# Wide products for every pair of parts two and three of a SwiGLU FFN, like products grouped, and the first corner cleared earlier

## The chip, the cores and the metric

One core of one Trainium2 chip runs the whole program. The metric is the device time of one execution in microseconds; three executions of the kernel before took 1763.86, 1764.16 and 1764.58 us, and their median, 1764.16 us, is what the change is compared with.

## The reference

Two layers of an encoder trunk on 512 tokens of width 1024, in float32. Each layer merges three token mixers, adds the result to x, and then runs the part that the change touches, a SwiGLU FFN (`D_FF` is 2816, so 22 blocks of 128 hidden channels), followed by a gated embedding:

```python
for i in range(DEPTH):
    h = rmsnorm(x, norm_mix[i])
    ...                                   # three mixers, merged; x = x + merged @ w_o[i]
    h = rmsnorm(x, norm_ffn[i])
    x = x + (jax.nn.silu(h @ w_ffn_gate[i]) * (h @ w_ffn_up[i])) @ w_ffn_down[i]
    h = rmsnorm(x, norm_ple[i])
    x = x + jax.nn.sigmoid(h @ w_ple_gate[i]) * (p[i] @ w_ple_in[i])
return rmsnorm(x, norm_final)
```

## The kernel before

**Arithmetic.** A float32 product is made of fp32r products: each operand is split into a high part (a copy in fp32r) and a low part (the rest), and a product is the sum of three, high weights with high activations, high weights with low activations, and low weights with high activations. ScalarE (ACT) makes the high part, VectorE (DVE) the low one (`split`, L143 and L157 for every operation of its kind). In a plain `gemm` the three are L179, L180 and L181, each 512 tokens wide.

**The FFN.** `ffn` goes through the 22 blocks `fb` in three parts, of 8, 7 and 7 blocks. For each block, a *pair* (gate block and up block), `seven` computes gate and up together by seven products in place of eight: the weights are taken as a 2x2 matrix (`a11`, `a12` of the gate block, sums `s1` to `s4`, `a22`), the activations as a 2x2 matrix too (`b11`, `b21`, `b22` and the differences `t1` to `t4`), over two halves of the channels and two halves of the 512 tokens. A product runs over four steps `k` of 128 channels and is 256 tokens wide. After a part's pairs, its block results go through the rows of `w_ffn_down` as plain gemms.

**Narrow and wide products.** In a pair with even `fb`, a product step is three matmuls of 256 columns (L1011, L1012, L1013), all into one 256-wide accumulator. In a pair with odd `fb` (`twice`), the high weights meet the high and the low activations in one matmul of 512 columns (L1008), into an accumulator of two halves, and the low weights meet the high activations in one of 256 columns (L1009) into the first half; the two halves are added when the accumulator is read. The product `T` (`s1` with `t3`) is narrow in every pair, so a wide pair has six wide products and a narrow one. Reading a two-half accumulator costs a copy on ACT and an addition on DVE that a narrow one doesn't have.

**Accumulators.** A pair has three in PSUM. `C` takes `a11 b11`; ACT copies it to `A`; `C` then takes `a12 b21` as well and is the first corner of the result (the gate for the first token half). `A` takes `s3 t2`, is copied by ACT to `Q`, takes `s2 t1`, is read out by ACT (`self.cleared`), and takes `s4 b22`; `Q` takes `a22 t4`. Even pairs hold three banks called `mm`, odd pairs two called `sc` and one called `av`, so a bank comes free for the next pair but one. The first pair of all (`fb` 0, `early`) does `s4 b22` apart.

**Order.** TensorE's (PE) order is written by hand: `sevens_of` runs two pairs interleaved, so that between `s2 t1` of a pair and its `s4 b22` stand two other products (its own `a22 t4`, and `T` of the next pair), and between its corner `a12 b21` and the next use of that bank, by `a11 b11` of the next pair but one, stand six. The other engines' orders come from the scheduler of the tile framework, by priority (weights are hoisted), with a few orders forced by `behind`. SP issues the weight DMAs, POOL the accumulating DMAs (L976) that form `s1` and `s2`. Tiles: `wr` raw weights, `wh` and `wl` their parts, `qk` the sums, `pt` and `y` the parts of `s3`, `s4` for even and odd pairs, `kh` and `a` those of `a22`, `t` results, `h`, `rp`, `b`, `v`, `z` the activations.

Of the kernel before, what the change touches and what calls it, by code (L numbers as in the profile page):

```python
# [20 lines left out]
P = 128  # L21
# [40 lines left out]
class Net:  # L62
# [212 lines left out]

    def norm_chunk(self, k, x, g, tag, st, n=512):

        if k == KD - 1:
            self.sumsq(k, x, st)
        if n < 512:  # L280
            tag = self.sb(tag, [P, 2, 512], F32R)[:, :, :n]
        h = self.operand(x[:, :n], g, tag)
        if k < KD - 1:
            self.sumsq(k, x, st)
        return h
# [616 lines left out]
    def w_o(self, mg, xsrc):  # L902
        self.phase = "wo"
        xs, h, st, self.four = [], [], [], []
        self.zs = [self.parts_of("z", [2, 256], 2, F32R) for _ in range(4)]
        for m in range(KD):
            if m % 2 == 0:
                two = self.parts_of("x", [512], 2)
            xo = two[m % 2]
            self.nc.sync.dma_start(xo, xsrc[m])  # L910
            if m == 0:
                both = [self.ps("mm") for _ in range(2)]
                self.pair(both, self.a["w_o"][self.i, 0:2], mg)
# [6 lines left out]
            h.append(self.norm_chunk(m, xo, self.par(self.i, "ffn", m), "h", st, 512 if m % 2 else 256))  # L920
# [40 lines left out]
    def seven(self, wg, wu, bs, tags, spare, md, first, fb, early, twice):  # L961


        nc = self.nc
        with self.tc.high_priority(offset=min(self.w_ahead, self.tc.cur_priority - self.p0)):
# [30 lines left out]
            self.tt(s4, s3, g[:, up], ALU.add)  # L996
            halve(*spare, sums[1], ("s3", "s4"))
        shape = (P, 2, 256) if twice else (P, 256)
        C, A, Q = (self.ps(t, shape) for t in tags)

        def product(out, w, b, first=False):
            wh, wl = ws[w]
            mm = nc.tensor.matmul
            for k in range(4):
                c = slice(k * P, k * P + P)
                both = bs[k][b]
                if len(out.shape) > 2:
                    mm(out, wh[:, c], both, start=first and k == 0, stop=False, skip_group_check=True)  # L1008
                    mm(out[:, 0], wl[:, c], both[:, 0], start=False, stop=k == 3, skip_group_check=True)  # L1009
                    continue  # L1010
                mm(out, wh[:, c], both[:, 0], start=first and k == 0, stop=False, skip_group_check=True)  # L1011
# [20 lines left out]
        product(T, "s1", "t3", True)  # L1032
        shared = gg[:, 1] if twice else uu[:, 0]
        self.act(shared, T, AF.Copy)
# [7 lines left out]
        if twice:  # L1042
            self.act(uu[:, 1], A[:, 0], AF.Copy)
            self.cleared = self.act(gg[:, 0], A[:, 1], AF.Copy)
        else:
            self.cleared = self.act(uu[:, 1], A, AF.Copy)
        product(Q, "a22", "t4")
        if twice:
            self.tt(uu[:, 1], uu[:, 1], gg[:, 0], ALU.add)
            self.act(uu[:, 0], Q[:, 1], AF.Copy)  # L1050
            self.tt(uu[:, 0], Q[:, 0], uu[:, 0], ALU.add)
            self.tt(uu, uu, gg[:, 1:2].to_broadcast([P, 2, 256]), ALU.add)
        else:
# [68 lines left out]
    def ffn(self, h, x):  # L1122
# [5 lines left out]
        md8 = [self.sb(t, [P, 2, 512], F32R) for t in ["v"] * 3 + ["z"] + ["y"] * 3]  # L1128
        md8.append(tuple(self.sb("e", [P, 512], F32R) for _ in range(2)))
        self.sums, self.sevens = [t for _ in range(2) for t in self.parts_of("qk", [1024], 2)], 0  # L1130
        for part in PARTS:
            mids = md8[:len(part)]
            self.sevens_of((self.seven(self.a["w_fg"][i, fb], self.a["w_fu"][i, fb], bs,
                                       (("mm", "mm", "mm"), ("sc", "sc", "av"))[fb % 2],
                                       spare[fb % 2], md8[f], part[0] and f < 2, fb, fb == 0,
                                       fb % 2 == 1)
                            for f, fb in enumerate(part)), part[0] == 0)
# [368 lines left out]
```

## Time and profile before

| what | value |
|---|---|
| three executions | 1763.86, 1764.16, 1764.58 us |
| profiled execution, its own time | 1764.9 us |
| its span on the core | 1763.1 us (1.8 us of the time lie outside it) |
| DVE busy in the span | 1388.2 us (79%) |
| ACT busy in the span | 934.6 us (53%) |
| granted TensorE clock | 0.999 |

The span holds three stretches of pairs in each layer, with the gemms of `w_ffn_down` behind each: in the first layer pairs of part one from 491 to 572.2 us, of part two from 615.8 to 685.6, of part three from 723.7 to 793.4; in the second layer each about 873 us later. Records of matmuls overlap, since they are pipelined: what a matmul costs is the distance from its start to the next one's, not its duration. In the rows below, a tile's name has its stage ahead of it (`ffn_mm`), and `out<-in` says what is written and from what.

### The profile page before, as it was taken

Reading aid. Unit: us, or ns where it says so; the run is one execution under the profiler, and the core shown is the slowest. Engines: PE = TensorE matmul, PEld = TensorE weight load, DVE = VectorE, ACT = ScalarE, POOL = GpSimd, SP = SyncE. Lnnn points to the kernel's source line nnn. Section 1 sums busy time; section 2 is a strip of 40 time slices with the busy share of each in tenths; the row PEclk is TensorE's granted clock in tenths of the full one; section 3 lists DMA queues with packets and bytes.
Section 4 is the critical chain, followed back from the end, with each engine's and each line's share of the span. In section 5 each row is a group of like instructions: output and inputs, shape, how many; then the busy total and the mean of one; then the engine's idle time right before and its main releaser. Section 6 shows DMA issues by size and latency. Waiting matters only on the chain.

```text
span 1763.1 us, 26202 instructions
## 1 busy us (share of the span) xinstructions
PE 1756.3 (100%) x9618; PEld 1525.2 (87%) x9618; DVE 1388.2 (79%) x2264; ACT 934.6 (53%) x1649; POOL 104.1 (6%) x114
## 2 busy tenths in 40 slices
PE   9999999999999999999999999999999999999998
PEld 7889888888899898898888888888888998989987
DVE  7967988998788676777776789889887875877776
ACT  5566555326576264464545655552356653645554
POOL 0000000000121020100000000000001210201000
PEclk9999999999999999999999999999999999999999
DMA  6565641334767365543445655322356664656332
GB/s 227 163 188 157 164 123 54 102 99 150 223 161 181 119 170 154 141 118 131 149 137 166 190 148 153 111 75 93 101 182 190 180 166 122 177 143 154 97 105 96
DMA packets 114785, 253.90 MB, mean 144 GB/s; under 512 B 16864, under 2 KB 23776, under 8 KB 114656
## 3 DMA queue, kind: packets, MB, share of 16 engines
q1 hardware_dynamic: 101264, 227.83, 41.9%
q0 software_dynamic: 12672, 23.07, 8.0%
q8 instruction: 76, 1.25, 0.3%
q10 hardware_dynamic: 720, 1.31, 0.2%
q14 instruction: 53, 0.43, 0.1%
HBM read 215.46 MB, written 7.34 MB: 126 GB/s over the span
## 4 chain that ended last, share of the span: by engine, by line
PE 99%; DVE 0%; ACT 0%; POOL 0%; issue 0%; POOLq 0%; ACTq 0%; DVEq 0%
PE ffn_sc L1008 6%; PE ffn_mm L179 4%; PE ffn_mm L180 4%; PE ffn_mm L181 4%; PE ffn_mm L1011 4%; PE ffn_mm L1013 4%; PE ffn_mm L1012 4%; PE ffn_sc L1009 3%; PE mergea_mm L179 2%; PE mergea_mm L181 2%; PE mergea_mm L180 2%; PE diff_sc L798 2%; PE diff_mm L179 2%; PE diff_mm L180 2%; PE gatec_mm L180 2%; PE natten_mm L180 2%
## 5 line engine op out<-in xcount | busy, mean ns | idle before, releaser
L160 DVE SCALAR_TENSOR_TENSOR conv_z<-glu_z,pre_par,conv_z 128x512 f32<-128x512 f32 x240 | 179.4, 748 | 3.4
L143 ACT ACTIVATE ffn_wh<-ffn_wr 128x1024 fp32r<-128x1024 f32 (+1 forms) x92 | 92.6, 1020 | 117.1 <-PE ffn_mm L180 61.4
L157 DVE TENSOR_TENSOR ffn_wl<-ffn_wr,ffn_wh 128x1024 fp32r<-128x1024 f32 (+1 forms) x92 | 107.1, 1175 | 40.2 <-ACT ffn_wh L143 39.7
L976 POOL DMA_DIRECT2D ffn_qk<-w_fu x88 | 78.0, 974 | 595.6 <-DMA ffn_qk<-w_fu 308.0
L157 DVE TENSOR_TENSOR ffn_t<-ffn_mm,wo_rb 128x512 f32<-128x512 f32 (+1 forms) x86 | 47.9, 557 | 55.1 <-PE ffn_mm L181 46.9
L143 ACT ACTIVATE mergea_wh<-mergea_wr 128x1024 fp32r<-128x1024 f32 (+1 forms) x32 | 27.1, 846 | 96.8 <-PE mergea_mm L180 79.5
L157 DVE TENSOR_TENSOR ffn_t<-ffn_t,ffn_t 128x512 f32<-128x512 f32 x88 | 54.4, 619 | 18.0 <-ACT ffn_t L143 18.0
L157 DVE TENSOR_TENSOR ffn_wl<-ffn_qk,ffn_wh 128x1024 fp32r<-128x1024 f32 x44 | 53.8, 1223 | 16.6 <-ACT ffn_wh L143 16.6
L1008 PE MATMUL ffn_sc<-wo_h,ffn_wh 128*128 128x512 f32 x176 | 64.2, 399 | 0.1
L143 ACT ACTIVATE ffn_wh<-ffn_qk 128x1024 fp32r<-128x1024 f32 x44 | 46.6, 1060 | 31.4 <-PE ffn_mm L180 16.2
L143 ACT ACTIVATE diff_a<-diff_sc,diff_s 128x512 f32<-128x512 f32 x32 | 22.1, 689 | 70.8 <-DVE diff_s L891 70.8
L181 PE MATMUL ffn_mm<-ffn_v,ffn_wl 128*128 128x512 f32 x132 | 51.4, 390 | 0.0
L180 PE MATMUL ffn_mm<-ffn_v,ffn_wh 128*128 128x512 f32 x132 | 51.4, 390 | 0.0
L179 PE MATMUL ffn_mm<-ffn_v,ffn_wh 128*128 128x512 f32 x132 | 51.3, 389 | 0.0
L179 PE MATMUL ffn_mm<-ffn_y,ffn_wh 128*128 128x512 f32 x132 | 51.3, 389 | 0.0
L180 PE MATMUL ffn_mm<-ffn_y,ffn_wh 128*128 128x512 f32 x132 | 51.3, 389 | 0.0
L181 PE MATMUL ffn_mm<-ffn_y,ffn_wl 128*128 128x512 f32 x132 | 51.3, 389 | 0.0
L1011 PE MATMUL ffn_mm<-wo_h,ffn_wh 128*128 128x256 f32 x176 | 50.0, 284 | 0.0
L1012 PE MATMUL ffn_mm<-wo_h,ffn_wh 128*128 128x256 f32 x176 | 49.8, 283 | 0.0
L1013 PE MATMUL ffn_mm<-wo_h,ffn_wl 128*128 128x256 f32 x176 | 49.8, 283 | 0.0
L1009 PE MATMUL ffn_sc<-wo_h,ffn_wl 128*128 128x256 f32 x176 | 49.5, 281 | 0.0
L143 ACT ACTIVATE natten_wh<-natten_wr 128x1024 fp32r<-128x1024 f32 x24 | 25.4, 1058 | 42.1 <-issue 15.2
(847 smaller groups left out, 6325.4 us busy)
## 6 DMA issues: line engine op xcount, KB each, us to landing
ffn_qk<-w_fu POOLq DMA_DIRECT2D x88, 256.0 KB, 6.3
ffn_wr<-w_fg SPq DMA_DIRECT2D x44, 512.0 KB, 4.4
ffn_wr<-w_fd SPq DMA_DIRECT2D x32, 448.0 KB, 4.0
ffn_r<-w_fu SPq DMA_DIRECT2D x44, 256.0 KB, 3.3
ffn_qk<-w_fg SPq DMA_DIRECT2D x44, 256.0 KB, 3.2
ffn_qk<-w_fu SPq DMA_DIRECT2D x44, 256.0 KB, 3.4
natten_wr<-w_in SPq DMA_DIRECT2D x16, 512.0 KB, 4.0
diff_wr<-w_in SPq DMA_DIRECT2D x16, 512.0 KB, 4.2
```

The source lines that it names most:

```text
L143: i = self.nc.scalar.activation(out, in_, func, **kw)
L157: return self.nc.vector.tensor_tensor(out, a, b, op)
L160: return self.nc.vector.scalar_tensor_tensor(out, a, s, b, op0, op1)
L179: mm(out, wh, ah, start=first, stop=False, **kw)
L180: mm(out, wh, al, start=False, stop=False, **kw)
L181: mm(out, wl, ah, start=False, stop=last, **kw)
L976: nc.gpsimd.dma_start(q, wu[:, lo], accum_op=ALU.add)
L1008: mm(out, wh[:, c], both, start=first and k == 0, stop=False, skip_group_check=True)
L1009: mm(out[:, 0], wl[:, c], both[:, 0], start=False, stop=k == 3, skip_group_check=True)
L1011: mm(out, wh[:, c], both[:, 0], start=first and k == 0, stop=False, skip_group_check=True)
L1012: mm(out, wh[:, c], both[:, 1], start=False, stop=False, skip_group_check=True)
L1013: mm(out, wl[:, c], both[:, 0], start=False, stop=k == 3, skip_group_check=True)
```

## The change

Four edits, all in the FFN.

1. `twice`, which makes a pair's products wide, is true for all pairs of parts two and three, and no longer only for odd `fb`. Those are 7 more pairs in each layer, 14 in all.
2. In a wide product the four matmuls of the high weights come first, one for each `k`, and then the four of the low weights. Before, the two kinds alternated.
3. A wide pair gets two side tiles (`side`, from the ring `e`) for the second half of `A` and for `T`. With these free, the first corner `C` is read out and added right behind its last product, where it was read at the pair's end together with `A`. The reading of `A` at the end is kept in `self.late`, and the low parts of `s3` and `s4` of the next pair but one are put behind it on DVE.
4. The normalised activations `h` are laid out as token half, then high or low, so that `b11`, `b21` and `b22` are each one contiguous piece of 512 columns; before they were two pieces of 256.

```diff
+            h.append(self.sb("h", [P, 2, 2, 256], F32R))
+            self.norm_chunk(m, xo, self.par(self.i, "ffn", m), h[m], st, m % 2 + 1)
...
-        return dict(b11=ha, b21=hb[:, :, one], b22=hb[:, :, two],
+        return dict(b11=ha[:, 0], b21=hb[:, 0], b22=hb[:, 1],
...
-            halve(*spare, sums[1], ("s3", "s4"))
+            i = halve(*spare, sums[1], ("s3", "s4"))
+            if self.late[fb % 2] is not None:
+                self.behind(i, self.late[fb % 2])
+                self.late[fb % 2] = None
...
-                if len(out.shape) > 2:
-                    mm(out, wh[:, c], both, start=first and k == 0, stop=False, skip_group_check=True)
-                    mm(out[:, 0], wl[:, c], both[:, 0], start=False, stop=k == 3, skip_group_check=True)
-                    continue
+            if len(out.shape) > 2:
+                for k, c in enumerate(cols):
+                    mm(out, wh[:, c], bs[k][b], start=first and k == 0, stop=False,
+                       skip_group_check=True)
+                for k, c in enumerate(cols):
+                    mm(out[:, 0], wl[:, c], bs[k][b][:, 0], start=False, stop=k == 3,
+                       skip_group_check=True)
...
         def corner():
             product(C, "a12", "b21")
-            if not early and not twice:
+            if twice:
+                self.act(gg[:, 0], C[:, 1], AF.Copy)
+                self.tt(gg[:, 0], C[:, 0], gg[:, 0], ALU.add)
+            elif not early:
                 self.tt(gg[:, 0], C, self.halved(0), ALU.mult)
...
-            self.cleared = self.act(gg[:, 0], A[:, 1], AF.Copy)
+            self.cleared = self.act(side[:, 1], A[:, 1], AF.Copy)
...
-            for n, o in enumerate((C, A)):
-                self.act(gg[:, n], o[:, 1], AF.Copy)
-                self.tt(gg[:, n], o[:, 0], gg[:, n], ALU.add)
+            self.act(gg[:, 1], A[:, 1], AF.Copy)
+            self.late[fb % 2] = self.tt(gg[:, 1], A[:, 0], gg[:, 1], ALU.add)
...
+        side = [self.sb("e", [P, 2, 256]) for _ in range(2)]
...
-                                       fb % 2 == 1)
+                                       fb, fb == 0, fb % 2 == 1 or part[0] > 0)
```

The first place is on PE, in part two: the product `s4 b22` of pair 10 into its accumulator `A` (`ffn_mm_1110_6464` before, `ffn_mm_1112_6432` now; `wo_h` are the activations, `ffn_pt` the parts of `s4`). Before:

```order
L1011 MATMUL ffn_mm_1110_6464<-wo_h_802_4422,ffn_pt_871_4766 128x256
L1012 MATMUL ffn_mm_1110_6464<-wo_h_802_4422,ffn_pt_871_4766 128x256
L1013 MATMUL ffn_mm_1110_6464<-wo_h_802_4422,ffn_pt_872_4767 128x256
L1011 MATMUL ffn_mm_1110_6464<-wo_h_822_4522,ffn_pt_871_4766 128x256
L1012 MATMUL ffn_mm_1110_6464<-wo_h_822_4522,ffn_pt_871_4766 128x256
L1013 MATMUL ffn_mm_1110_6464<-wo_h_822_4522,ffn_pt_872_4767 128x256
L1011 MATMUL ffn_mm_1110_6464<-wo_h_844_4625,ffn_pt_871_4766 128x256
L1012 MATMUL ffn_mm_1110_6464<-wo_h_844_4625,ffn_pt_871_4766 128x256
L1013 MATMUL ffn_mm_1110_6464<-wo_h_844_4625,ffn_pt_872_4767 128x256
L1011 MATMUL ffn_mm_1110_6464<-wo_h_862_4725,ffn_pt_871_4766 128x256
L1012 MATMUL ffn_mm_1110_6464<-wo_h_862_4725,ffn_pt_871_4766 128x256
L1013 MATMUL ffn_mm_1110_6464<-wo_h_862_4725,ffn_pt_872_4767 128x256
```

Now, with the lines of the changed kernel (L1013 is the wide matmul, L1016 the narrow one):

```order
L1013 MATMUL ffn_mm_1112_6432<-wo_h_802_4422,ffn_pt_871_4766 128x512
L1013 MATMUL ffn_mm_1112_6432<-wo_h_822_4522,ffn_pt_871_4766 128x512
L1013 MATMUL ffn_mm_1112_6432<-wo_h_844_4625,ffn_pt_871_4766 128x512
L1013 MATMUL ffn_mm_1112_6432<-wo_h_861_4722,ffn_pt_871_4766 128x512
L1016 MATMUL ffn_mm_1112_6432<-wo_h_802_4422,ffn_pt_872_4767 128x256
L1016 MATMUL ffn_mm_1112_6432<-wo_h_822_4522,ffn_pt_872_4767 128x256
L1016 MATMUL ffn_mm_1112_6432<-wo_h_844_4625,ffn_pt_872_4767 128x256
L1016 MATMUL ffn_mm_1112_6432<-wo_h_861_4722,ffn_pt_872_4767 128x256
```

Twelve matmuls of 256 columns have become four of 512 and four of 256; the columns that stream are the same 3072. All in all PE has 336 matmuls fewer (84 products, four fewer in each).

The second place is on ACT, in part two, around the reading of pair 8's `A` (`ffn_mm_1082_6230` before, `ffn_mm_1084_6216` now) ahead of its `s4 b22`. Before:

```order
L143 ACTIVATE ffn_sc_1096_6351<-ffn_sc_1095_6350 128x512
L143 ACTIVATE ffn_wh_1103_6447<-ffn_wr_1101_6439 128x1024
L143 ACTIVATE ffn_v_876_4771<-ffn_t_1070_6119 128x512
L143 ACTIVATE ffn_kh_1105_6451<-ffn_r_1102_6440 128x512
L143 ACTIVATE ffn_t_1085_6233<-ffn_mm_1082_6230 128x256
L143 ACTIVATE ffn_t_1098_6353<-ffn_tr_1100_6391 128x256
```

Now, for the same pair:

```order
L143 ACTIVATE ffn_sc_1098_6324<-ffn_sc_1097_6323 128x512
L143 ACTIVATE ffn_wh_1105_6415<-ffn_wr_1103_6407 128x1024
L143 ACTIVATE ffn_v_876_4771<-ffn_t_1072_6110 128x512
L143 ACTIVATE ffn_kh_1107_6419<-ffn_r_1104_6408 128x512
L143 ACTIVATE ffn_t_1087_6219<-ffn_mm_1084_6216 128x256
L143 ACTIVATE ffn_e_884_4779<-ffn_mm_1084_6216 128x256
L143 ACTIVATE ffn_t_1087_6219<-ffn_mm_1085_6217 128x256
L143 ACTIVATE ffn_e_885_4780<-ffn_tr_1102_6359 128x256
```

The four operations ahead of the reading of `A` are the same; the reading itself is now two copies, and a copy of the second half of `Q` stands behind them.

The third place is on DVE at the beginning of the first layer's FFN, between the reading of pair 1's accumulators and the parts of pair 2's and 3's weights (`ffn_sc_913_4911` is pair 1's `C` before, `ffn_sc_915_4913` now). Before:

```order
L157 TENSOR_TENSOR ffn_wl_938_5127<-ffn_wr_935_5118,ffn_wh_937_5126 128x1024
L157 TENSOR_TENSOR ffn_t_917_4915<-ffn_t_917_4915,ffn_t_916_4914 128x256
L157 TENSOR_TENSOR ffn_pt_872_4767<-ffn_qk_885_4780,ffn_pt_871_4766 128x1024
L157 TENSOR_TENSOR ffn_a_940_5131<-ffn_r_936_5119,ffn_kh_939_5130 128x512
L157 TENSOR_TENSOR ffn_qk_885_4780<-ffn_qk_884_4779,ffn_r_936_5119 128x512
L157 TENSOR_TENSOR ffn_t_917_4915<-ffn_av_915_4913,ffn_t_917_4915 128x256
L157 TENSOR_TENSOR ffn_qk_885_4780<-ffn_qk_885_4780,ffn_wr_935_5118 128x512
L157 TENSOR_TENSOR ffn_t_917_4915<-ffn_t_917_4915,ffn_t_916_4914 128x512
L157 TENSOR_TENSOR ffn_t_916_4914<-ffn_sc_913_4911,ffn_t_916_4914 128x256
```

Now:

```order
L157 TENSOR_TENSOR ffn_t_918_4916<-ffn_sc_915_4913,ffn_t_918_4916 128x256
L157 TENSOR_TENSOR ffn_qk_887_4782<-ffn_qk_887_4782,ffn_wr_923_5001 128x512
L157 TENSOR_TENSOR ffn_wl_940_5129<-ffn_wr_937_5120,ffn_wh_939_5128 128x1024
L157 TENSOR_TENSOR ffn_a_942_5133<-ffn_r_938_5121,ffn_kh_941_5132 128x512
L157 TENSOR_TENSOR ffn_pt_872_4767<-ffn_qk_887_4782,ffn_pt_871_4766 128x1024
L157 TENSOR_TENSOR ffn_t_919_4917<-ffn_t_919_4917,ffn_e_885_4780 128x256
L157 TENSOR_TENSOR ffn_qk_887_4782<-ffn_qk_886_4781,ffn_r_938_5121 128x512
```

The reading of pair 1's `C` has moved from the last of these rows to the first, ahead of pair 3's first weight parts; and pair 2's low part of `s3` and `s4` (`ffn_pt_872`) now stands behind `ffn_a`, the low part of `a22`, where it stood ahead of it. The DMA issues of SP and POOL stand in the same order as before.

More of the change, by code (lines that the diff above doesn't have):

```diff
@@ L957, in quarters, with seven @@
         ha, hb = h[2 * j], h[2 * j + 1]
-        return dict(b11=ha, b21=hb[:, :, one], b22=hb[:, :, two],
+        return dict(b11=ha[:, 0], b21=hb[:, 0], b22=hb[:, 1],
                     **{f"t{n + 1}": o for n, o in enumerate(d)})
-    def seven(self, wg, wu, bs, tags, spare, md, first, fb, early, twice):
+    def seven(self, wg, wu, bs, tags, spare, side, md, first, fb, early, twice):
         nc = self.nc
@@ L1032, in seven @@
         product(T, "s1", "t3", True)
-        shared = gg[:, 1] if twice else uu[:, 0]
+        shared = side[:, 0] if twice else uu[:, 0]
         self.act(shared, T, AF.Copy)
@@ L1134, in ffn @@
                                        (("mm", "mm", "mm"), ("sc", "sc", "av"))[fb % 2],
[L1135 to L1136 removed]
+                                       spare[fb % 2], side[fb % 2], md8[f], part[0] and f < 2,
+                                       fb, fb == 0, fb % 2 == 1 or part[0] > 0)
                             for f, fb in enumerate(part)), part[0] == 0)
```

20 lines of the change are left out of this document (11 added, 9 removed).

## The prediction

> **What bounds the kernel now.** I read the page's span and its chain of waits first.
>
> ```profile
> span 1763.1 us, 26202 instructions
> ...
> PE 99%; DVE 0%; ACT 0%; POOL 0%; issue 0%; POOLq 0%; ACTq 0%; DVEq 0%
> ```
>
> The chain that ended last lies on PE for 99% of the span, so what counts is how far apart matmuls start. I read that next from windows with exact borders, in the first layer: the gemms behind part one, then the pairs of part two, then those of part three.
>
> ```profile
> core 0: us, PE busy (x) PEld busy (x) DVE busy (x) ACT busy (x) POOL busy (x), PEclk, DMA share, GB/s
> 572.23:615.78 43.55, 43.55 (x194) 36.04 (x193) 27.97 (x37) 12.14 (x16) 0.00 (x0) 1.00 0.37 120
> 615.79:685.62 69.83, 69.83 (x517) 66.54 (x516) 54.30 (x82) 45.50 (x79) 12.40 (x14) 1.00 0.68 167
> 723.74:793.37 69.63, 69.63 (x493) 65.25 (x492) 52.80 (x80) 45.31 (x80) 7.04 (x8) 1.00 0.51 134
> ```
>
> The counts in brackets include one or two matmuls that cross a border; by the code they are 192, 516 and 492. The 192 of the gemms have 512 columns each: 43.55 / 192 = 226.8 ns. Part two has four narrow pairs and three wide ones: 4 x 84 + 3 x 12 = 372 narrow matmuls, and 3 x 24 = 72 steps of a wide and a narrow one. Part three has 3 x 84 + 4 x 12 = 300 and 96. With n for a narrow matmul and p for a wide-and-narrow step, 372 n + 72 p = 69.83 and 300 n + 96 p = 69.63, so n = 119.8 ns and p = 351.0 ns. The timeline shows a wide product in single rows, from 565.19 to 566.60:
>
> ```profile
> 565.19 0.40 PE L1008 MATMUL ffn_sc<-wo_rp,ffn_y 128*128 128x512 f32 x1
> 565.42 0.28 PE L1009 MATMUL ffn_sc<-wo_rp,ffn_y 128*128 128x256 f32 x1
> 565.54 0.40 PE L1008 MATMUL ffn_sc<-wo_rp,ffn_y 128*128 128x512 f32 x1
> 565.78 0.28 PE L1009 MATMUL ffn_sc<-wo_rp,ffn_y 128*128 128x256 f32 x1
> 565.90 0.40 PE L1008 MATMUL ffn_sc<-wo_z,ffn_y 128*128 128x512 f32 x1
> 566.14 0.28 PE L1009 MATMUL ffn_sc<-wo_z,ffn_y 128*128 128x256 f32 x1
> 566.25 0.40 PE L1008 MATMUL ffn_sc<-wo_z,ffn_y 128*128 128x512 f32 x1
> ...
> 566.60 0.40 PE L1008 MATMUL ffn_sc<-wo_h,ffn_wh 128*128 128x512 f32 x1
> ```
>
> From n and the gemms, 256 more columns cost 226.8 - 119.8 = 107 ns, so that a matmul costs 12.8 ns beside its columns. That is all a wide product can save, since the columns stay the same.
>
> **Term 1, 84 products become wide.** A narrow product is 12 x 119.8 = 1437.6 ns, a wide one as it is now 4 x 351.0 = 1404.0 ns. 14 pairs x 6 products x 33.6 ns = **2.8 us less**.
>
> **Term 2, like matmuls grouped, in 132 + 84 = 216 wide products.** A wide-and-narrow step takes 351.0 ns where 226.8 + 119.8 = 346.6 would do: alternating costs 4.4 ns a step. Grouped, a product alternates once and not four times: 3 x 4.4 = 13.2 ns, x 216 = **2.9 us less**; if that once goes too, 3.8 us. On the bad side, the rows let the excess be the wide matmul's own: three wide ones start 0.23, 0.24 and 0.24 us ahead of their narrow ones (236.7 ns mean), and three narrow ones take 0.12, 0.12 and 0.11. If wide ones keep 236.7 ns and narrow ones in a row take 119.8, a product is 1426 ns, 22 ns more than now, 4.8 us in all. I take 2.9, because the gemms' matmuls, of the same size and in a row, hold 226.8 ns over 192 of them.
>
> **The operands in one piece: nothing.** The half-and-half `wo_h` and the one-piece `wo_rp` take the same already:
>
> ```profile
> L1008 PE MATMUL ffn_sc<-wo_h,ffn_wh x176: 387/398/468, 498.6 to 1662.0; 128*128 128x512 f32 x176
> L1008 PE MATMUL ffn_sc<-wo_rp,ffn_wh x44: 393/397/404, 509.1 to 1662.7; 128*128 128x512 f32 x44
> ```
>
> **Term 3, the waits at the FFN's beginning.** PE waits twice in a layer in its first 30 us of pairs, and not behind that:
>
> ```profile
> 517.55 0.28 PE L1013 MATMUL ffn_mm<-wo_h,ffn_wl 128*128 128x256 f32 x1
> 517.86 0.47 PE L1008 MATMUL ffn_sc<-wo_h,ffn_wh 128*128 128x512 f32 x1
> ...
> 523.50 0.28 PE L1013 MATMUL ffn_tr<-wo_z,ffn_wl 128*128 128x256 f32 x1
> 523.79 0.39 PE L1011 MATMUL ffn_mm<-wo_h,ffn_pt 128*128 128x256 f32 x1
> ```
>
> ```profile
> 513.42 1.22 DVE L157 TENSOR_TENSOR ffn_pt<-ffn_qk,ffn_pt 128x1024 fp32r<-128x1024 f32 x1
> ...
> 517.29 0.42 DVE L157 TENSOR_TENSOR ffn_t<-ffn_sc,ffn_t 128x256 f32<-128x256 f32 x1
> ```
>
> The first (0.31 us between starts where 0.12 is usual, and 0.07 more in the longer matmul: 0.26) is pair 3's first product, which needs the bank of pair 1's `C`: DVE reads that at 517.29 and is done at 517.71. Early clearing puts this reading some six us ahead (the third place in the order), so the wait goes. The second (0.29 for 0.12, and 0.11 in the matmul: 0.28) is pair 2's `s4 b22`, which needs `A` read by ACT; in the new order the copy and the Silu that delayed ACT stand ahead of it, and I let it go too. What is late next is the low part of `s3` for pair 2: it ends at 514.64, and its first reader starts at 515.03:
>
> ```profile
> 515.03 0.29 PE L1013 MATMUL ffn_mm<-wo_rp,ffn_pt 128*128 128x256 f32 x1
> ```
>
> That is 0.39 us of room, and the new order puts the low part of `a22` ahead of it (0.60 us from start to start; the addition of 0.33 that stood there has gone behind, the reading of `C` of 0.33 has come ahead). I take a new wait of 0.14, between 0 and 0.3. A layer gains 0.26 + 0.28 - 0.14 = 0.40, two layers **0.8 us**; ends 0 and 1.1.
>
> **What is added beside PE.** Each of the 14 pairs gets two additions of 256 columns turned into ones of 512 and two more of 256 on DVE, on ACT four more copies of 256 and two that grow to 512. The groups of part two give the prices (417 and 685 ns; on ACT 378 and 582):
>
> ```profile
> L157 DVE TENSOR_TENSOR ffn_t<-ffn_sc,ffn_t 128x256 f32<-128x256 f32 x6 | 2.5, 417 | 0.5 <-ACT ffn_t L143 0.5
> L157 DVE TENSOR_TENSOR ffn_t<-ffn_t,ffn_t 128x512 f32<-128x512 f32 x9 | 6.2, 685 | 0.8 <-ACT ffn_t L143 0.8
> L143 ACT ACTIVATE ffn_t<-ffn_sc 128x256 f32<-128x256 f32 x12 | 4.2, 378 | 2.5 <-DVE ffn_t L157 1.5 <-PE ffn_sc L1009 1.1
> L143 ACT ACTIVATE ffn_sc<-ffn_sc 128x512 f32<-128x512 f32 x3 | 1.7, 582 | 0.4 <-PE ffn_sc L1009 0.4
> ```
>
> DVE: 2 x 0.417 + 2 x 0.268 = 1.37 us a pair, in part two 54.30 + 4 x 1.37 = 59.8 of 69 us, 87%. ACT: 4 x 0.378 + 2 x 0.204 = 1.92, 45.50 + 7.7 = 53.2 of 69, 77%. Neither becomes the pace; PE's work hides them, and it costs nothing as long as no product waits. The low parts of `s3` and `s4`, now forced behind the reading of `A`, are due late: in the steady part DVE makes them some seven us ahead of use. DMA issues keep their order.
>
> The tightest place is the reading of `A` by ACT ahead of `s4 b22`, in the steady part:
>
> ```profile
> 644.06 0.28 PE L1012 MATMUL ffn_mm<-wo_z,ffn_wh 128*128 128x256 f32 x1
> ...
> 647.15 0.28 PE L1011 MATMUL ffn_mm<-wo_h,ffn_pt 128*128 128x256 f32 x1
> ```
>
> ```profile
> 644.38 1.06 ACT L143 ACTIVATE ffn_wh<-ffn_wr 128x1024 fp32r<-128x1024 f32 x1 [0.55 <-PE ffn_mm L1012]
> 645.35 0.62 ACT L143 ACTIVATE ffn_v<-ffn_t 128x512 fp32r<-128x512 f32 x1
> 645.87 0.62 ACT L143 ACTIVATE ffn_kh<-ffn_r 128x512 fp32r<-128x512 f32 x1
> 646.39 0.36 ACT L143 ACTIVATE ffn_t<-ffn_mm 128x256 f32<-128x256 f32 x1
> ...
> 655.36 0.64 ACT L143 ACTIVATE ffn_t<-ffn_sc 128x256 f32<-128x256 f32 x2
> ```
>
> The last high matmul of `s2 t1` (644.06 to 644.34) frees the buffer that ACT then fills with the next high weights (644.38), behind which stand three more operations; `A` is free at 646.75, and PE wants it at 647.15: 0.40 us of room. Now, from the start of the last high matmul: it lasts 0.40, so ACT starts at +0.44, the first copy of `A` 2.01 later, and both copies take 0.64 (the row of two at 655.36): free at +3.09. PE wants `A` when `s2 t1` has ended, four narrow matmuls and one wide later (0.71), and `a22 t4` (1.39) and `T` (1.44) have run: +3.54. The room is 0.45 us. No wait is added.
>
> **The sum.** 2.8 + 2.9 + 0.8 = 6.5 us less. The rows are those of one execution of 1764.9 us (its span 1763.1 and 1.8 around it), which becomes 1758.4; the median of the runs, 1764.16, lies 0.7 lower, and I take the same 6.5 from it: **1757.7 us**. The ends of the terms are 7.7 less (1756.5) and 2.8 - 4.8 + 0 = 2.0 more (1766.2).
>
> **Rivals.** *Grouping brings nothing*, because the 4.4 ns belong to the pair of matmuls on the same columns and not to the change of width. For: no row before shows wide matmuls of this form in a row. Against: the gemms' 226.8. It leaves 2.8 + 0.8: 1760.6 us. Chance 0.19.
>
> *Columns alone set the pace*: merging two matmuls then saves nothing, and grouping neither; only term 3 stays, 1763.4 us. Against it stands n: 119.8 is more than half of 226.8, and p less than 3 n. Chance 0.06. The Trainium skill (TensorE: Matmul & The Clock Gate, Back-to-back issue gap) comes close to this case: it states a gap of N / 2.4 + 2.5 ns for a warm matmul, so 2.5 ns beside the columns. By that, an estimate from the page, term 1 would be 84 x 4 x 2.5 ns = 0.84 us, and the time 1762.5 us with term 3. The trace differs, with 12.8 ns.
>
> *`A` is read too late* in the 28 pairs of parts two and three of both layers: now two copies must be through before `s4 b22`. If ACT's first operation of the chain starts later, by more than 0.45 us, PE waits in every pair. If another hi part of 1024 columns (0.97 us from 644.38 to 645.35) gets ahead, each pair waits 0.97 - 0.45 = 0.52, 28 x 0.52 = 14.6 us: 1772.3 us. It decides against the change from a slip of 0.45 + 6.5 / 28 = 0.68 us. For: ACT goes from 65% to 77%, and the room is small. Against: the order of ACT at this place is the old one with one more copy. Chance 0.11.
>
> **How the numbers follow.** The forecast (1757.7, its own range 1756 to 1759.5) has 0.64. The range of 8 in 10 takes in the first rival with some tenths above it for a small new wait, and leaves out the late reading, most of the second rival and the bad end of term 2: 1755.8 to 1762.6 us. A measurement of this kernel can tell about 0.2%, 3.5 us, from no change: under 1760.6 counts as faster. That holds all of the forecast and half of the first rival's cases, 0.64 + 0.09 = 0.73; the other half and the second rival make 0.16 for the same; the third makes 0.11 for slower.
>
> **What would show it.** In the changed profile: windows over the pairs of parts two and three shorter by 4 x 6 x 33.6 ns = 0.8 and by 0.6 us from term 1, and by 42 x 13.2 ns = 0.55 each from term 2, so 68.5 for 69.83 and 68.5 for 69.63; wide matmuls in a row 0.227 apart and narrow ones 0.120; no gap of PE near 517.9 and 523.8, a small one near 515; DVE near 60 us busy in part two. Wide ones that stay at 0.235 would make term 2 wrong, a PE gap ahead of each `s4 b22` the account of ACT.

## The result and the profile after

The changed kernel takes 1758.43 us (median of six runs, 1757.92 to 1759.2), beside 1764.69 us (1763.86 to 1765.18) for the kernel before in six runs: a ratio of 0.9966 with a 95% interval of 0.9957 to 0.9976, 6.3 us less. The profiled execution took 1758.65 us, its span 1756.9.

The page's first line and its chain of waits, for the changed kernel:

```profile
span 1756.9 us, 25630 instructions
...
PE 99%; DVE 0%; ACT 0%; POOL 0%; issue 0%; POOLq 0%; ACTq 0%; DVEq 0%
```

PE still makes the whole chain. The stretches, as windows with exact borders (from the start of a stretch's first matmul to the start of the next stretch's), in the first layer: part one from 500.5 us on (ahead of that, other work stands between its products), part two, part three. Part one of the kernel before:

```profile
500.52:572.22 71.70, 71.66 (x511) 67.08 (x509) 59.22 (x90) 49.09 (x87) 12.39 (x14) 1.00 0.75 184
```

The changed kernel:

```profile
core 0: us, PE busy (x) PEld busy (x) DVE busy (x) ACT busy (x) POOL busy (x), PEclk, DMA share, GB/s
500.48:571.34 70.86, 70.86 (x511) 66.86 (x509) 59.78 (x91) 49.00 (x88) 12.37 (x14) 1.00 0.75 186
614.89:683.57 68.68, 68.68 (x421) 61.38 (x420) 57.67 (x88) 50.66 (x93) 12.40 (x14) 1.00 0.72 170
721.68:790.37 68.69, 68.69 (x421) 61.41 (x420) 57.14 (x87) 50.19 (x92) 7.08 (x8) 1.00 0.52 135
```

Part one is 0.84 us shorter, part two 1.16 (69.84 before), part three 0.95 (69.64); the second layer's stretches agree with the first's within 0.05 us. That is 2.95 us a layer, 5.9 in all; the other 0.3 us between the two spans lie outside the pairs. The gemms behind the parts kept their lengths. DVE is busy for 57.7 of 68.7 us in part two (59.8 were forecast), ACT for 50.7 (53.2), and PE doesn't wait for them: apart from the first matmul of part one, 0.08 us late before and after the change, no distance between matmuls in these stretches is more than some 25 ns over the usual.

PE's timeline in part two, one row for each run of like matmuls (the count stands at the end), shows `s2 t1`, `a22 t4`, `T` and the beginning of `s4 b22`:

```profile
641.52 0.62 PE L1013 MATMUL ffn_mm<-wo_rp,ffn_wh 128*128 128x512 f32 x2
641.98 0.62 PE L1013 MATMUL ffn_mm<-wo_z,ffn_wh 128*128 128x512 f32 x2
642.45 0.40 PE L1016 MATMUL ffn_mm<-wo_rp,ffn_wl 128*128 128x256 f32 x2
...
642.92 0.39 PE L1013 MATMUL ffn_mm<-wo_v,ffn_kh 128*128 128x512 f32 x1
...
644.32 0.28 PE L1020 MATMUL ffn_tr<-wo_v,ffn_wh 128*128 128x256 f32 x1
...
645.74 1.09 PE L1013 MATMUL ffn_mm<-wo_h,ffn_pt 128*128 128x512 f32 x4
```

`s2 t1` runs from 641.52 to 642.92 and `a22 t4` to 644.32: 1.40 us each. Its four wide matmuls take 642.45 - 641.52 = 0.93, or 232 ns apiece, its four narrow ones 0.47, or 118. `T`, twelve narrow ones, takes 1.42. Over all wide products that stand between two wide ones in parts two and three, 108 of them, the mean from start to start is 1399.8 ns.

ACT's timeline at the place where the prediction saw the tightest room, the same pair:

```profile
642.65 1.06 ACT L143 ACTIVATE ffn_wh<-ffn_wr 128x1024 fp32r<-128x1024 f32 x1 [0.28 <-PE ffn_mm L1013]
643.61 0.62 ACT L143 ACTIVATE ffn_v<-ffn_t 128x512 fp32r<-128x512 f32 x1
644.13 0.62 ACT L143 ACTIVATE ffn_kh<-ffn_r 128x512 fp32r<-128x512 f32 x1
644.65 0.37 ACT L143 ACTIVATE ffn_t<-ffn_mm 128x256 f32<-128x256 f32 x1
644.92 0.37 ACT L143 ACTIVATE ffn_e<-ffn_mm 128x256 f32<-128x256 f32 x1
```

`A` is free at 644.92 + 0.37 = 645.29 and wanted by `s4 b22` at 645.74 (above): 0.45 us of room, the 0.45 that was forecast.

The waits at the FFN's beginning are gone. These are the places of the prediction's two waits, in the changed kernel:

```profile
517.43 0.28 PE L1022 MATMUL ffn_mm<-wo_h,ffn_wl 128*128 128x256 f32 x1
517.55 1.09 PE L1013 MATMUL ffn_sc<-wo_h,ffn_wh 128*128 128x512 f32 x4
...
523.11 0.28 PE L1022 MATMUL ffn_tr<-wo_z,ffn_wl 128*128 128x256 f32 x1
523.23 0.28 PE L1020 MATMUL ffn_mm<-wo_h,ffn_pt 128*128 128x256 f32 x1
```

0.12 us between starts at both, as everywhere; and the new wait that was expected near 515 did not come.

### The profile page after: what moved, and what is told of

Same layout as the page of the kernel before. It is cut to its first block, busy times and chain, and to the rows that moved or that the text cites. A ratio compares the mean times of both kernels' runs of the same rounds, so it can differ in the third digit from the quotient of the medians.

```text
span 1756.9 us, 25630 instructions
## 1 busy us (share of the span) xinstructions
PE 1750.2 (100%) x9282; PEld 1507.1 (86%) x9282; DVE 1405.9 (80%) x2292; ACT 954.5 (54%) x1705; POOL 104.0 (6%) x114
## 4 chain that ended last, share of the span: by engine, by line
PE 99%; DVE 0%; ACT 0%; POOL 0%; issue 0%; POOLq 0%; ACTq 0%; DVEq 0%
PE ffn_sc L1013 6%; PE ffn_mm L1013 4%; PE ffn_mm L180 4%; PE ffn_mm L181 4%; PE ffn_mm L179 4%; PE ffn_sc L1016 3%; PE mergea_mm L181 2%; PE mergea_mm L180 2%; PE mergea_mm L179 2%; PE ffn_mm L1016 2%; PE diff_sc L800 2%; PE diff_mm L180 2%; PE diff_mm L179 2%; PE gatec_mm L180 2%; PE natten_mm L179 2%; PE gatec_mm L179 2%
## 5 line engine op out<-in xcount | busy, mean ns | idle before, releaser
L157 DVE TENSOR_TENSOR ffn_t<-ffn_mm,wo_rb 128x512 f32<-128x512 f32 (+1 forms) x58 | 36.1, 623 | 51.1 <-PE ffn_mm L181 51.1
L1013 PE MATMUL ffn_sc<-wo_h,ffn_wh 128*128 128x512 f32 x176 | 47.8, 393 | 0.0
L893 DVE TENSOR_REDUCE diff_s<-diff_sc 128x1 f32<-128x512 f32 x64 | 42.1, 681 | 2.2 <-PE diff_sc L800 2.2
L157 DVE TENSOR_TENSOR ffn_t<-ffn_t,ffn_t 128x512 f32<-128x512 f32 x44 | 30.2, 686 | 15.0 <-ACT ffn_t L143 15.0
L225 POOL TENSOR_TENSOR diff_rc<-diff_sm,pre_power 128x4 f32<-128x4 f32 x8 | 8.9, 1116 | 561.1 <-DVE diff_sm L160 502.6
L157 DVE TENSOR_TENSOR ffn_t<-ffn_t,ffn_e 128x256 f32<-128x256 f32 x72 | 39.9, 554 | 2.4 <-ACT ffn_e L143 1.4
L143 ACT ACTIVATE natten_b<-natten_b,natten_s 128x256 f32<-128x256 f32 x64 | 30.4, 500 | 20.3 <-DVE natten_s L719 20.3
```

The costliest lines, as they stand in the source:

```text
L143: i = self.nc.scalar.activation(out, in_, func, **kw)
L157: return self.nc.vector.tensor_tensor(out, a, b, op)
L225: nc.gpsimd.tensor_tensor(col, ms, self.power, ALU.pow)
L893: nc.vector.tensor_reduce(out=m[:, u:u + 1], in_=sc, op=ALU.max, axis=AX.X, negate=True)
L1013: mm(out, wh[:, c], bs[k][b], start=first and k == 0, stop=False, skip_group_check=True)
```

## The experiments

All times are compared with the kernel before on the same chip, 1764.57 to 1764.61 us in the three sets of runs. Stretches are those of the first layer, PE's part one / two / three; before 71.70 / 69.84 / 69.64, changed 70.86 / 68.68 / 68.69.

### One part undone or done alone

**Grouping undone** (the changed kernel, its wide products alternating again):

```diff
                 for k, c in enumerate(cols):
                     mm(out, wh[:, c], bs[k][b], start=first and k == 0, stop=False,
                        skip_group_check=True)
-                for k, c in enumerate(cols):
                     mm(out[:, 0], wl[:, c], bs[k][b][:, 0], start=False, stop=k == 3,
                        skip_group_check=True)
```

> The changed kernel with the matmuls of a wide product alternating again (a wide one, a narrow one, for each k). If grouping is worth only its own streaming: the changed profile's pairs of part two last 68.69 us, a wide product 1.396 us; alternating it is 1.404 us as before the change, so 42 x 8.3 ns = 0.35 us more in each of parts two and three, 0.2 in part one, 1.8 us in all, and no new wait of PE. If grouping also buys room for the reading of A (the last matmul on the high weights then ends earlier and ACT starts earlier): without it the room of 0.45 us ahead of s4 b22 shrinks by 0.36 us to about 0.1, and PE may begin to wait there in each wide pair, up to 0.1 us x 28 = 2.8 us on top.

Measured: 1761.7 us, ratio 0.9983 (0.9975 to 0.9992); 71.48 / 69.32 / 69.35. The mean wide product between wide ones, where PE doesn't wait, takes 1409.4 ns and not 1399.8: 9.6 ns for the order of the matmuls, 216 x 9.6 = 2.1 us. The rest are waits that the changed kernel doesn't have: of 45 to 65 ns at `s4 b22` in four pairs of part two and four of part three, one of 0.09 us in part one, and one at the FFN's beginning (PE):

```profile
514.35 0.28 PE L1020 MATMUL ffn_mm<-wo_rp,ffn_pt 128*128 128x256 f32 x1
514.61 0.39 PE L1021 MATMUL ffn_mm<-wo_rp,ffn_pt 128*128 128x256 f32 x1
514.84 0.28 PE L1019 MATMUL ffn_mm<-wo_rp,ffn_pt 128*128 128x256 f32 x1
```

From 514.35 to 514.84 lie 0.49 us where 0.24 are usual. That is pair 2's low part of `s3`, the new wait of the prediction. All these waits make 0.8 us a layer. By the stretches the kernel loses 1.92 us a layer, 3.8 in all, and by the medians 3.3; the two profiled executions differ ahead of the FFN too, where part one starts at 499.97 and at 500.48 us.

**Grouping alone** (the kernel before with its own 132 wide products grouped):

> The kernel before, with the matmuls of the wide products of odd pairs grouped and nothing else changed. If grouping is worth 8.3 ns a product as the stretches of the changed kernel suggest: 132 products, 1.1 us less than before; with the 13.2 ns of the prediction 1.7 us less; if the 8.3 ns come from something else in the change, 0. The two waits of PE at the beginning of the FFN should stay, about 0.5 us in each layer, since they hang on when C and A are read.

Measured: 1762.81 us, ratio 0.999 (0.9981 to 0.9999); 71.42 / 69.57 / 69.31. Part two loses 0.27 us for 18 products, part three 0.33 for 24, some 14 ns each. In part one, against the expectation, both of the prediction's waits go (0.04 us is left of that of pair 3's first product), and a new one stands ahead of pair 5:

```profile
537.14 0.28 PE L1016 MATMUL ffn_mm<-wo_h,ffn_wl 128*128 128x256 f32 x1
537.69 0.93 PE L1007 MATMUL ffn_sc<-wo_h,ffn_wh 128*128 128x512 f32 x3 [0.27 <-DVE ffn_t L157]
```

**Wide products alone** (the kernel before, nothing else changed):

```diff
-                                       fb % 2 == 1)
+                                       fb % 2 == 1 or part[0] > 0)
```

> The kernel before, with all pairs of parts two and three wide and nothing else changed: no side tiles, C read at the pair's end, products not grouped. If the parts of the change are independent: 84 products x 33.6 ns = 2.8 us less than before. If wide pairs need the early reading of C: with every pair wide, DVE reads C and A of each pair behind the large operations at the pair's end, and the bank of C is wanted two products later; PE then waits ahead of the first product of pairs, 0.26 us (as at the beginning of the FFN before) to 0.8 us, in 14 to 28 pairs: 3.6 to 20 us more, which eats the 2.8 or more than that.

Measured: 1768.51 us, ratio 1.0022 (1.0012 to 1.0031): slower, 71.68 / 70.84 / 70.94, though 84 products are cheaper. PE, DVE and ACT at the place of it:

```profile
641.52 0.28 PE L1009 MATMUL ffn_mm<-wo_h,ffn_wl 128*128 128x256 f32 x1
642.34 0.47 PE L1008 MATMUL ffn_sc<-wo_h,ffn_wh 128*128 128x512 f32 x1 [0.55 <-DVE ffn_t L157]
```

```profile
639.25 0.42 DVE L157 TENSOR_TENSOR ffn_t<-ffn_t,ffn_t 128x256 f32<-128x256 f32 x1
...
640.64 1.22 DVE L157 TENSOR_TENSOR ffn_y<-ffn_qk,ffn_y 128x1024 fp32r<-128x1024 f32 x1
641.78 0.75 DVE L157 TENSOR_TENSOR ffn_t<-ffn_sc,ffn_t 128x256 f32<-128x256 f32 x2
```

```profile
639.42 1.06 ACT L143 ACTIVATE ffn_y<-ffn_qk 128x1024 fp32r<-128x1024 f32 x1 [1.50 <-DVE ffn_qk L157]
640.39 0.37 ACT L143 ACTIVATE ffn_t<-ffn_sc 128x256 f32<-128x256 f32 x1
```

The odd pair's first product wants the bank of `C` (`ffn_sc`) at 641.64 and gets it at 642.34. The copy of `C` goes into the half of `gg` that still holds the second half of `A`, which DVE reads at 639.25; so ACT's copy stands behind the high part of `s3`, `s4` (`ffn_y`, until 640.39), and DVE's addition behind their low part, at 641.78. Eight such waits, two in part two and two in part three of each layer, make this kernel slower than the one before.

**The reading of C at the end again** (the changed kernel without the early clearing; side tile, `late` and grouping kept):

```diff
-            if twice:
+            if not early and not twice:
-                self.act(gg[:, 0], C[:, 1], AF.Copy)
-                self.tt(gg[:, 0], C[:, 0], gg[:, 0], ALU.add)
-            elif not early:
                 self.tt(gg[:, 0], C, self.halved(0), ALU.mult)
...
         if twice:
+            self.act(gg[:, 0], C[:, 1], AF.Copy)
+            self.tt(gg[:, 0], C[:, 0], gg[:, 0], ALU.add)
             self.act(gg[:, 1], A[:, 1], AF.Copy)
```

> The changed kernel, with C of wide pairs read at the pair's end together with A again; the side tiles, the grouping and the order of DVE behind the reading of A stay. If the early reading matters only at the beginning of the FFN: that stretch gets back the wait for the bank of C, 0.26 us in each layer, 0.5 us more in all than the changed kernel. If it matters in every pair: PE waits ahead of first products in parts two and three as well, 0.26 us or more x 14 to 28, 3.6 us or more.

Measured: 1758.64 us, ratio 0.9965 (0.9952 to 0.9979); 70.88 / 68.69 / 68.68. Nothing is lost but 0.03 us a layer at pair 3's first product. So it was not the early clearing that took away the third experiment's waits; the next two ask what did.

**Wide products and the side tile alone.** The same kernel as the third experiment, with `T` and the second half of `A` copied to `side`:

```diff
-        shared = gg[:, 1] if twice else uu[:, 0]
+        shared = side[:, 0] if twice else uu[:, 0]
...
-            self.cleared = self.act(gg[:, 0], A[:, 1], AF.Copy)
+            self.cleared = self.act(side[:, 1], A[:, 1], AF.Copy)
...
```

> The kernel before with two edits: all pairs of parts two and three wide (as in e3_wide_only), and the side tile for the copies of T and of A's second half. No grouping, no early clearing of C, no order behind the reading of A, operands as before. Theory S (the side tile alone frees C's reading: without it the sum of C on DVE has to wait until the copies of T and A that lie in the same tile gg have been read): the 0.7 us gaps of PE ahead of an odd pair's first product go, parts two and three come down from 70.84 and 70.95 to the ungrouped kernel's 69.3 each, small waits ahead of s4 b22 stay; the time is about 1761.8 us, ratio 0.998. Rival C (the early clearing of C, or the order behind the reading of A, is what removes them): the gaps stay, parts two and three stay at 70.8 to 71.0, 1768.5 us, ratio 1.002.

Measured: 1761.83 us, ratio 0.9984 (0.9975 to 0.9993); 71.57 / 69.45 / 69.47. The waits of 0.7 us are gone. ACT's and DVE's rows at the same place:

```profile
638.60 0.38 ACT L143 ACTIVATE ffn_t<-ffn_sc 128x256 f32<-128x256 f32 x1 [0.94 <-PE ffn_sc L1009]
638.96 1.06 ACT L143 ACTIVATE ffn_y<-ffn_qk 128x1024 fp32r<-128x1024 f32 x1
```

```profile
639.51 0.41 DVE L157 TENSOR_TENSOR ffn_t<-ffn_sc,ffn_t 128x256 f32<-128x256 f32 x1
...
640.44 1.22 DVE L157 TENSOR_TENSOR ffn_y<-ffn_qk,ffn_y 128x1024 fp32r<-128x1024 f32 x1
```

The reading of `C` now stands ahead of both `ffn_y`, though no line of the program asks for it: with a place to go, the scheduler puts it there. What stays are the small waits ahead of `s4 b22`, here in ACT's and then in PE's rows:

```profile
644.13 1.06 ACT L143 ACTIVATE ffn_wh<-ffn_wr 128x1024 fp32r<-128x1024 f32 x1
...
646.14 0.37 ACT L143 ACTIVATE ffn_t<-ffn_mm 128x256 f32<-128x256 f32 x1
646.40 0.38 ACT L143 ACTIVATE ffn_e<-ffn_mm 128x256 f32<-128x256 f32 x1
```

```profile
642.64 0.40 PE L1008 MATMUL ffn_mm<-wo_rp,ffn_wh 128*128 128x512 f32 x1
...
646.89 0.44 PE L1008 MATMUL ffn_mm<-wo_h,ffn_pt 128*128 128x512 f32 x1
647.17 0.28 PE L1009 MATMUL ffn_mm<-wo_h,ffn_pt 128*128 128x256 f32 x1
```

`A` is free at 646.78, 0.1 us ahead of the product, whose first matmul then takes 0.28 us to the next and not 0.23; the changed kernel has 0.45 of room. `s2 t1` starts at 642.64 here, and ACT's chain 1.49 us behind it, at 644.13, once the last high matmul has freed the weights' buffer; in the changed kernel it is 1.13 us (641.52 to 642.65).

**With grouping added to that.** The edit is the diff of the change's second part.

> As e5_wide_side, with like products grouped in all wide products. Against the changed kernel it lacks the early clearing of C, the order behind the reading of A, and the operands in one piece. Theory S+G (streaming, the side tile and grouping are all that counts): parts two and three 68.7 us each, as in the changed kernel; part one within 0.2 us of its 70.87; 1758.5 to 1759 us, ratio 0.9968. Rival: one of the three that are left out is worth something, then a part stays over 69.0 us, or the time over 1760 us.

Measured: 1758.94 us, ratio 0.9967 (0.9955 to 0.998):

```profile
501.20:572.09 70.89, 70.89 (x511) 66.90 (x509) 59.03 (x90) 48.96 (x87) 12.39 (x14) 1.00 0.76 187
615.64:684.33 68.69, 68.69 (x421) 61.40 (x420) 56.70 (x87) 50.16 (x92) 12.43 (x14) 1.00 0.71 170
```

Those are the changed kernel's stretches within 0.03 us. Wide products, the side tile and grouping are the whole gain; early clearing, the order behind the reading of `A` and the operands in one piece add nothing that these runs can show but the 0.03 to 0.04 us at pair 3's first product.

### Why a grouped wide matmul costs 232 ns and not 227

The pitch, in what follows, is the distance from a matmul's start to the next one's.

**The gemms, ordered by kind.** In the changed kernel, each gemm of eight blocks runs the high weights with the high activations for all blocks, then with the low ones, then the low weights, so that, as in a grouped product, neighbours share neither weights nor operand:

```diff
+            hs = [self.halves(acts[o + k]) for k in range(c)]
+            for turn, (w, n2) in enumerate(((wh, 0), (wh, 1), (wl, 0))):
+                for k in range(c):
+                    s = slice(k * P, (k + 1) * P)
+                    self.nc.tensor.matmul(out, w[:, s], hs[k][n2],
...
```

> The changed kernel, where each gemm of eight blocks runs the high products with the first operand for all blocks, then those with the second, then the low ones (now the three of a block follow one another and two of them share their weights). Only the order of matmuls of 512 columns changes. Theory O (wide matmuls take 231 instead of 227 ns where no neighbour shares weights or operand): the gemms behind the parts go from 227 to 231 ns a matmul, the 43.56 us behind part one to about 44.2, all gemms some 20 us more. Rival P (it belongs to the products, not to the order): 226 to 228 ns as before. New waits at the gemms' borders are possible, where an operand is wanted in another order; the pitch is read away from them.

PE in a gemm behind part one:

```profile
586.52 0.84 PE L193 MATMUL ffn_mm<-ffn_v,ffn_wh 128*128 128x512 f32 x3
...
590.14 0.84 PE L193 MATMUL ffn_mm<-ffn_v,ffn_wl 128*128 128x512 f32 x3
```

16 matmuls in 590.14 - 586.52 = 3.62 us, 226 ns each. Theory O falls. (The time, 1766.82 us in one run, holds new waits at borders, the largest 1.4 us in the mixers.)

**The low matmuls left out of the wide products**, so that 24 wide ones follow one another:

```diff
-                    mm(out, wh[:, c], bs[k][b], start=first and k == 0, stop=False,
-                       skip_group_check=True)
-                for k, c in enumerate(cols):
-                    mm(out[:, 0], wl[:, c], bs[k][b][:, 0], start=False, stop=k == 3,
+                    mm(out, wh[:, c], bs[k][b], start=first and k == 0, stop=k == 3,
                        skip_group_check=True)
```

> The changed kernel without the four low matmuls of each wide product, so that six wide products, 24 matmuls of 512 columns, follow one another between two narrow products T (wide products lack the term of the low weights). Theory M (what costs is the beginning of a row of wide matmuls behind narrow ones: about 233, 236, 228, 232, 231 ns for the first five, as at the beginning of the gemms behind the parts, and 227 from the sixth on): behind T the first five look like that, the others 226 to 228, wherever PE does not wait. Rival P (wide matmuls of the products cost 231 to 232 whatever stands before them): 231 to 232 all along the row. PE has a third less to do in the pairs, so new waits for ACT and DVE come; the pitch is read between them, the time is no answer (estimate: 84 products less 4 x 119.8 ns in parts two and three of both layers and 48 in part one, at most 63 us less).

Measured: 1715.71 us in one run. In 31 rows the first wide matmul stands directly behind a narrow one and PE doesn't wait. There the first six take 232.5, 233.6, 231.1, 230.9, 231.2 and 230.1 ns in the mean (31 rows for the first three, 29 for the fourth, 24 for the others), and those from the seventh to the fourth from the end 226.6. (Five short stretches of this run have a granted clock of 0.5; none of these matmuls lies in them.) The beginning of one row on PE, and ahead of it four wide matmuls of a pair that follow a gemm's wide ones:

```profile
607.53 0.39 PE L181 MATMUL ffn_mm<-ffn_e,ffn_wl 128*128 128x512 f32 x1
607.75 1.07 PE L1013 MATMUL ffn_mm<-wo_h,ffn_wh 128*128 128x512 f32 x4
608.66 0.28 PE L1017 MATMUL ffn_tr<-wo_v,ffn_wh 128*128 128x256 f32 x1
...
610.08 0.62 PE L1013 MATMUL ffn_mm<-wo_rp,ffn_pt 128*128 128x512 f32 x2
...
611.00 1.08 PE L1013 MATMUL ffn_mm<-wo_h,ffn_wh 128*128 128x512 f32 x4
611.92 1.07 PE L1013 MATMUL ffn_sc<-wo_h,ffn_wh 128*128 128x512 f32 x4
612.83 0.62 PE L1013 MATMUL ffn_mm<-wo_rp,ffn_wh 128*128 128x512 f32 x2
```

Behind the gemm, the pair's four take 608.66 - 607.75 = 0.91 us, 227 ns each, at once. Behind the twelve narrow ones of `T`, the first eight take 611.92 - 610.08 = 1.84 us, 230 ns each, and the next four 0.91, 227 each. All of them have the products' own weights, operands and banks. So theory M holds: it is the beginning of a row behind narrow matmuls that costs. The end costs something too: in 14 of the 24 long rows the last three take 233 or 234, 225 or 226, and 235 or 236 ns. The changed kernel's gemm behind part one begins in the same way, behind narrow matmuls without a wait: 233, 236, 228, 233 and 230 ns, and then 227. A group of four ends before the pitch has settled.

### Further along the same road

**Part one's even pairs wide too**, and then **`T` wide as well**:

```diff
-                                       fb, fb == 0, fb % 2 == 1 or part[0] > 0)
+                                       fb, fb == 0, fb > 0)
...
-        T = self.ps("tr", (P, 256))
+        T = self.ps("tr", shape)
...
-        self.act(shared, T, AF.Copy)
+        self.act(shared, T[:, 1] if twice else T, AF.Copy)
+        if twice:
+            self.tt(shared, T[:, 0], shared, ALU.add)
```

> The changed kernel, where part one's pairs 2, 4 and 6 are wide too. 18 products a layer at 1396 ns for 1437.6: 0.75 us a layer, 1.5 us in all, if no new wait comes: part one's rest 70.87 to 70.1, 1757.0 us, ratio to before 0.9957. Rival: part one has the quarters and the down of DVE's time beside it, and a wait for A or C takes it back: 1758.5 us or more.

> As e8_even_wide, and T wide too, in a bank of 512 columns of which ACT copies one half and DVE adds the other. 21 products a layer at 1396 to 1400 ns for 1437.6: 0.8 to 0.87 us a layer, 1.6 to 1.7 us in all against e8_even_wide: part one's rest 70.23 to 69.95, parts two and three 68.69 to 68.4, 1755.4 us, ratio to before 0.9948. Rival: DVE, that gets one addition of 0.42 us more in each pair, is at some 90% of the pairs' time, and a wait for it takes back 0.1 us or more in each pair: 1757 us or more.

The first takes 1757.04 us, ratio 0.9957 (0.9945 to 0.997), its part one 70.23 us, without a new wait. The second takes 1756.01 us, ratio 0.9952 (0.9938 to 0.9965):

```profile
500.73:570.77 70.04, 70.04 (x411) 61.68 (x410) 64.58 (x104) 54.12 (x100) 12.33 (x14) 1.00 0.74 188
614.33:682.79 68.46, 68.46 (x393) 59.97 (x392) 59.17 (x95) 50.57 (x93) 12.40 (x14) 1.00 0.70 173
```

Seven `T` of part two give 0.22 us, 31 ns each. The forecast of 0.29 was too high, since a narrow `T` among wide products costs 1419.5 ns (mean of 28 in the changed kernel) and not the 1437.6 it was reckoned at. By that alone, seven `T` would give 0.15; the rest lies in the other products, which take some 1.5 ns less each. No wait came, with DVE at 64.6 of 70.0 us. Both are under the changed kernel's 1758.43 by their medians; the intervals of the ratios overlap, and only the stretches show the gain plainly.

## Why the prediction came out

**What bounds the kernel** held: PE, by the distance of its matmuls.

**Term 1** was 2.8 us for 84 wide products. Wide products with the side tile, and nothing else, are 2.76 us under the kernel before by the medians (1761.83 and 1764.59). That is no proof of the size: the profiled execution, the slowest of the eleven, has new waits, and its stretches are only 1.4 us shorter. The matmuls alone can be read from parts two and three of the first experiment, which have the same products: without their eight waits (0.45 us) they last 138.2 us a layer, 1.26 less than before, 2.5 us in all. So the term was right in kind and 0.3 too large. A step of wide and narrow was reckoned at 351.0 ns, 1404 a product, from two equations that differ little from one another; single products show 1409.4. The narrow one, reckoned at 1437.6, is 1419.5 where it is `T` between wide products.

**Term 2** was 2.9 us for grouping, of which 216 x 13.2 ns were to come from the stream of matmuls. On top of wide products and side tile it brought 1761.83 - 1758.94 = 2.9 us, and undoing it in the changed kernel cost 3.3. But the stream's share is 9.6 ns a product, 2.1 us (2.3 by the stretches): the step that failed is "I take 2.9, because the gemms' matmuls, of the same size and in a row, hold 226.8 ns over 192 of them". They hold it from the sixth or seventh of a row on, and a group has four. (In the second experiment grouping brings some 14 ns a product: 11 of them in the wide products themselves, 3 in the narrow ones beside them.) The rest of what grouping brings in these experiments is waits, which the term had not counted: with the high matmuls first, the weights' buffer is free earlier, ACT starts its chain earlier, and `A` is read earlier. In parts two and three the kernel before has no such waits; wide products bring them, and grouping keeps them away.

**Operands in one piece: nothing.** The sixth experiment has them in two, with the same stretches.

**Term 3** was 0.8 us for two waits gone less a new one, so it was 0.3 too small. Both waits are gone and the new one did not come: part one lost 0.84 us a layer, of which 24 products at 9.6 to 14 ns, 0.23 to 0.34, are the stream; 0.5 to 0.6 is left, 1.0 to 1.2 us in all. The account of it was only half of the story. Without early clearing the first wait is gone as well, in the fourth and sixth experiments; with neither early clearing nor grouping, in the fifth, it is there, 0.31 us from start to start:

```profile
517.62 0.28 PE L1013 MATMUL ffn_mm<-wo_h,ffn_wl 128*128 128x256 f32 x1
517.93 0.47 PE L1008 MATMUL ffn_sc<-wo_h,ffn_wh 128*128 128x512 f32 x1
```

Early clearing without grouping (the first experiment) takes it away too and lets the wait near 515 come, as the prediction had it, 0.25 us where it said 0.14. Grouping removes both; with it, pair 1's `C`, late in the fifth and the sixth alike, is read 0.3 us earlier from the part's start (517.67 - 501.20 in the sixth, 517.37 - 500.60 in the fifth). The second of the prediction's waits is still there in the third experiment (0.29 us between starts) and gone in the first, second, fourth, fifth and sixth, so the side tile alone removes it, and grouping alone too. In the fifth, ACT copies pair 3's `C` (`ffn_sc<-ffn_sc`) at 519.59, ahead of the next high weights at 520.90; before, that copy stood at 521.82, between these weights and the reading of `A`. In the changed kernel the Silu (`ffn_t<-ffn_t`) has gone ahead too (518.64), as the prediction had it; in the fifth it stays behind (521.87), and the copy alone is enough. The prediction reckoned each edit at that place by itself, and grouping only by the stream.

**The late reading of `A`**, the rival on the slow side, had its point of decision right: 0.45 us of room forecast, 0.45 found, and 0.1 in the kernel that doesn't group, which waits. What the prediction did not see is how near another wait was: in the third experiment, where the copies of `T` and `A` stay in `gg`, `C` is read late and the kernel is slower than before. (Whether grouping would make up for that, no run shows.) The prediction named the side tiles' operations one by one and their prices, but not what the tile was there to release.

**Columns alone** is ruled out by the fifth experiment: 2.76 us less with the same columns. The Trainium skill (TensorE: Matmul & The Clock Gate, Back-to-back issue gap) states N / 2.4 + 2.5 ns for an isolated warm matmul; by that, an estimate from the page, 512 columns would take 215.8 ns. The rows of wide matmuls here, which follow one another, settle at 226 to 227, so the trace doesn't agree.

**The sum**, 6.5 us, met 6.3, in part by luck. In the stretches, wide products make 2.5 us, grouping 2.3 and the two waits 1.1: 5.9 in all. The first two were forecast 0.3 and 0.6 too large, the third 0.3 too small, and the other 0.3 us between the spans lie outside the pairs, where the prediction had nothing.

## What to carry to other kernels

When an operation is made cheaper on the bound engine at the price of more reading beside it, ask first where the extra results go: here a scratch half that was shared between two accumulators turned a gain of 2.8 us into a loss of 3.9, by the scheduler's order and not by any engine's load. Order matmuls so that those that free a buffer come first; here that kept away waits of 0.8 to 1.2 us by the medians (1.5 to 2.4 by the stretches), beside 2.1 in the stream. And take the price of a row from a row of the same length: the mean over 192 hides what its beginning costs.

## What the hardware showed

A row of 512-column fp32r matmuls that begins directly behind 256-column ones starts slow: the first six take 230 to 234 ns in the mean, and from the seventh on they take 226.6 (ninth experiment). Behind other 512-column matmuls they take 226 and 227 at once. The order of weights and operands doesn't matter for the settled pitch (226 in the gemms ordered by kind). Why the beginning is slow is open. Other engines' work doesn't show in it: in the changed kernel's groups, the first wide matmul takes 230.8 ns where DVE and ACT are nearly idle (12 cases) and 230.5 where both are busy (80), the fourth 229.7 (6) and 228.7 (46); the second and third never had both idle. Behind the wide matmuls of a group, the four narrow ones take 117, 118, 119 and 120 ns in the mean.
